# Which instruction carries a wait: the last store's and the kernel's end's waits rearranged on SyncE in a row-sum kernel

## The chip, the cores and the metric

One core of one Trainium2 chip runs the kernel. The metric is device microseconds of a run. A run's span, as the profile shows it, is some 1.8 us shorter (160.8 us of span at 162.61 us in the profiled run before); only differences matter here. The record marks each run as fast or slow by its time and granted clock; all runs quoted are fast, at a granted clock of 1.0.

The engines that matter are VectorE (DVE in the profile), ScalarE (ACT) and SyncE (SP), which issues every DMA. "SPq" in a profile line is SyncE's sequencer. A nop is an instruction that does no work, used here to carry waits; a drain stands at the kernel's end, where it waits too, and the closing barrier is where all engines meet before the kernel ends.

## The reference

```python
batch, seq, dim = 32, 512, 1024        # x: float32, 64 MiB
def reference(x, multiplier):          # multiplier = 0.5
    return (np.sum(x, axis=-1) * multiplier).astype(np.float32)
```

There are 16384 rows of 1024 numbers in, 16384 numbers out.

## The kernel before

Each of 128 partitions owns 128 rows, handled in 8 blocks of 16. Seven blocks are one 8 MB load each into one of three buffers; VectorE sums half the rows, ScalarE the other half. The last block is loaded in five pieces, so that little work is left when the last bytes land. Results of the first 112 rows per partition (this is the 112-row pitch; it is in both kernels) go out in an early store, the last 16 in a last store. The part that matters is the end:

```python
    cut = 640
    ...                                           # pieces of the last block, the final row in two:
    for lo, hi in ((0, cut), (cut, D)):
        loads.append(nc.sync.dma_start(out=t[:, B - 1, lo:hi], in_=x_last[:, B - 1, lo:hi]))
    nc.sync.dma_start(out=out_rows, in_=res[:, 0:own])          # early store, 112 rows
    on_act = {4, 5, 6, 7, 11, 12, 14}
    for r in range(B - 1):
        ...                                       # ScalarE or VectorE, one row each
    dve_span(t, B - 1, 0, cut, part)              # partial sum of the final row
    dve_span(t, B - 1, cut, D, res[:, rows - 1 : rows], start=part)   # the last sum

    seen = nc.sync.nop()                          # waits for the loads and the last ScalarE row
    for i in loads[-8:] + acts[-1:]:
        tc.add_manual_dep(seen.ins, i.ins.name, ...Sync..., reason="ends seen early")
    store = nc.sync.dma_start(out=out_last, in_=res[:, own:])   # last store, 16 rows
    tc.add_manual_dep(store.ins, seen.ins.name, ...NoSync..., reason="in this order")
```

An instruction that depends on several others must wait for several semaphores. In the built program each instruction carries at most one or two waits, and the others stand in separate semaphore instructions ahead of it. The Trainium skill, "Perfetto Trace Analysis", section "Identifying Dependency Chains", says that such instructions may be inserted; this program agrees: six stand between the early store and the last one. It matters which wait stands where, because the program puts them there by its own order, not by which ends last. The end of SyncE's program before, each wait in brackets:

```
semaphore instr.  [load 5]
semaphore instr.  [load 6] [load 4]
semaphore instr.  [load 7] [last load]
semaphore instr.  [ScalarE's last row] [load 2]
semaphore instr.  [VectorE's last sum] [load 1]     <- the wait that ends last
semaphore instr.  [load 5] [load 0]
last store        [ScalarE's last row]
branch
semaphore instr.  [last store landed] [early store landed]
drain             [VectorE's last sum]
drain             enters the closing barrier of all engines
```

(A load is numbered by its semaphore. The pieces of the last block use the first loads' semaphores again, so loads 0, 1 and 2 stand here for pieces of the last block that land before the last load.)

## Time and profile before

| | before |
|---|---|
| median of the first three runs | 162.62 us (162.53 to 162.68) |
| moved by DMA | 67.18 MB, mean 418 GB/s |
| VectorE, ScalarE busy | 42%, 42% |
| chain that ended last | loads of x 86%, VectorE's reductions 11% |

First the table of stretches (core 0; length, busy us of each engine and its number of instructions, clock, DMA share, GB/s):

```profile
40.00:80.00 40.00, 17.75 (x5) 16.85 (x32) 0.00 (x0) 1.00 1.03 446
80.00:120.00 40.00, 18.71 (x5) 17.80 (x33) 0.00 (x0) 1.00 0.97 420
...
157.90:160.80 2.90, 0.50 (x4) 0.00 (x0) 0.00 (x0) 1.00 0.03 3
```

The 16 DMA engines are full, so the loads set the pace up to 157.9 us. The Trainium skill, "Perfetto Trace Analysis", section "Roofline", gives about 435 GB/s as what the 16 DMA engines of a core move together; this trace's mean of 418 GB/s is near it. (The 446 GB/s and the share of 1.03 in one stretch come from the view's counting a packet whole where it starts; with each packet spread over its own time, the trace gives 434 GB/s and a share of 1.00 there.) In the last 2.9 us almost nothing is moved: VectorE is busy for half a microsecond of it, and the DMA share is 0.03.

The timeline of that tail (start us, duration us, engine, line, operation, operands, count):

```profile
157.47 0.49 DVE L65 CUSTOM_DVE_ANT_0 xb<-xb 128x320 f32<-128x320 f32 x1
...
157.89 0.08 DVE L65 DVE_READ_ACCUMULATOR2_ANT part<- 128x1 f32 x1
158.02 0.42 DVE L65 CUSTOM_DVE_ANT_0 xb<-xb,part 128x192 f32<-128x192 f32 x1
158.37 0.08 DVE L65 DVE_READ_ACCUMULATOR2_ANT res<- 128x1 f32 x1
158.60 0.34 SPq L129 DMA_DIRECT2D out_dram<-res  x1
```

VectorE is done at 158.45, the store starts at 158.60. The instructions of the store's own line say what lies between (duration in ns as min/median/max, first and last start):

```profile
L129 SPq EVENT_SEMAPHORE  x2: 28/28/28, 158.5 to 158.5; - x2
L129 SPq DMA_DIRECT2D out_dram<-res x1: 344/344/344, 158.6 to 158.6; - x1
```

Two semaphore instructions stand behind VectorE's end. The view of SyncE's waits shows the wait that ends last at the kernel's end (us, times, longest):

```profile
SPq L194 <- DMA out_dram<-res: 1.1, 1, 1.1
...
SPq L129 <- DVE res L65: 0.5, 1, 0.5
```

The views print hundredths of a microsecond or tenths; the trace's records hold nanoseconds. They are given in tables below, in us from the span's start. A "start" is the record of an instruction's start, an "increment" or "landing" the record of the semaphore event.

### The profile page before, as it was taken

What the parts mean: (1) busy time and instruction counts of PE and PEld (TensorE: products, weight loads), DVE (VectorE), ACT (ScalarE), POOL (GpSimd) and SP (SyncE); (2) the same over time, 40 slices, a digit from 0 to 9 for tenths busy, and PEclk for the clock granted to TensorE, in tenths of its full rate; (3) what the DMA queues carried; (4) which work ended last, traced back from release to release, by engine and by line L of the source; (5) the groups of instructions that cost most, each with busy time, mean ns of one, the idle gap of its engine ahead of it and who ended that gap; (6) DMA issues with size and microseconds to landing.
All of it is one profiled execution on the core that took longest, in us unless ns stands there. A gap on an engine that the chain in (4) does not pass through costs nothing.

```text
span 160.8 us, 236 instructions
## 1 busy us (share of the span) xinstructions
DVE 68.1 (42%) x34; ACT 67.9 (42%) x127; POOL 0.2 (0%) x4
## 2 busy tenths in 40 slices
DVE  0000059600794009920199002990049700597453
ACT  3000059500793009910099002980039700596952
POOL 0000000000000000000000000000000000000000
DMA  7996996996996996996996996996996996998990
GB/s 261 522 522 261 522 522 261 522 522 261 522 522 261 522 522 261 522 522 261 522 524 261 522 505 277 522 505 277 522 505 277 522 489 293 408 489 381 413 390 23
DMA packets 2017, 67.18 MB, mean 418 GB/s; under 512 B 480, under 2 KB 608, under 8 KB 736
## 3 DMA queue, kind: packets, MB, share of 16 engines
q1 hardware_dynamic: 2016, 67.18, 97.3%
q14 instruction: 1, 0.01, 0.0%
HBM read 67.11 MB, written 0.07 MB: 418 GB/s over the span
## 4 chain that ended last, share of the span: by engine, by line
DMA 86%; DVE 11%; SPq 1%; issue 0%; DVEq 0%
DMA xb<-in_x_dram 86%; DVE sums L81 11%; SPq L99 1%; DVE xb L65 1%; SPq L79 0%; DVE part L65 0%; DVEq L194 0%
## 5 line engine op out<-in xcount | busy, mean ns | idle before, releaser
L55 ACT ACTIVATE xb<-xb 128x1024 f32<-128x1024 f32 x63 | 65.6, 1042 | 88.2 <-DMA xb<-in_x_dram 88.2
L81 DVE TENSOR_REDUCE sums<-xb 128x8 f32<-128x8192 f32 x7 | 60.8, 8686 | 85.0 <-DMA xb<-in_x_dram 85.0
L55 ACT ACTIVATION_READ_ACCUMULATOR xb<-xb 128x1 f32 x63 | 11.8, 187 | 0.0
L65 DVE CUSTOM_DVE_ANT_0 xb<-xb 128x512 f32<-128x512 f32 (+1 forms) x9 | 5.6, 667 | 5.1 <-DMA xb<-in_x_dram 4.9
L55 ACT ACT_TABLE_LOAD x1 | 1.3, 1283 | 1.7 <-PEq L180 1.7
L84 DVE TENSOR_SCALAR res<-sums 128x8 f32<-128x8 f32 x7 | 1.2, 171 | 0.2
L65 DVE DVE_READ_ACCUMULATOR2_ANT res<- 128x1 f32 x9 | 0.7, 83 | 0.0
L65 DVE CUSTOM_DVE_ANT_0 xb<-xb,part 128x192 f32<-128x192 f32 x1 | 0.4, 419 | 0.1
L180 POOL MEMSET const-bfloat16-1.0<- 128x1 bf16 x1 | 0.1, 101 | 0.0
L180 POOL MEMSET const-uint8-127<- 128x1 uint8 x1 | 0.1, 101 | 0.0
L180 POOL MEMSET const-float32-0.0<- 128x1 f32 x1 | 0.1, 98 | 0.2 <-issue 0.2
L180 POOL MEMSET const-float32-1.0<- 128x1 f32 x1 | 0.1, 98 | 0.0
L65 DVE DVE_READ_ACCUMULATOR2_ANT part<- 128x1 f32 x1 | 0.1, 83 | 0.0
## 6 DMA issues: line engine op xcount, KB each, us to landing
xb<-in_x_dram SPq DMA_DIRECT2D x1, 4096.0 KB, 39.6
xb<-in_x_dram SPq DMA_DIRECT2D x1, 2560.0 KB, 45.4
xb<-in_x_dram SPq DMA_DIRECT2D x1, 1024.0 KB, 47.4
xb<-in_x_dram SPq DMA_DIRECT2D x1, 320.0 KB, 47.7
xb<-in_x_dram SPq DMA_DIRECT2D x1, 192.0 KB, 47.7
xb<-in_x_dram SPq DMA_DIRECT2D x7, 49.6
out_dram<-res SPq DMA_DIRECT2D x1, 56.0 KB, 10.8
out_dram<-res SPq DMA_DIRECT2D x1, 8.0 KB, 1.4
```

Source lines behind the costliest of these rows:

```text
L55: acts.append(nc.scalar.activation(out=t[:, r, :], in_=t[:, r, :], func=mybir.ActivationFunctionType.Copy, scale=mul, accum_out=res[:, col ...
L65: nc.vector.tensor_tensor_reduce(out=t[:, r, lo:mid], in0=t[:, r, lo:mid], in1=t[:, r, mid:hi], scale=mul, scalar=start, op0=ADD, op1=ADD, ...
L81: nc.vector.reduce_sum(out=sums[:, c0 : c0 + h], in_=t[:, 0:h, :], axis=mybir.AxisListType.X)
L84: nc.vector.tensor_single_scalar(out=res[:, c0 : c0 + h], in_=sums[:, c0 : c0 + h], scalar=mul, op=mybir.AluOpType.mult,)
L99: nc.sync.dma_start(out=t[:, lo:hi, :], in_=x_last[:, lo:hi, :])
L180: nc = _bacc.Bacc("TRN2", target_bir_lowering=False, num_devices=1)
```

## The change

Intent: after the wait that ends last, no other instruction should stand on SyncE before the store, and none before the end's drain. The store is told that it need not wait for ScalarE again (the nop in front has), so that VectorE's wait is the one it carries. A second nop, behind the store, takes the end's other waits while the store is on its way.

```diff
+    def nop_after(engine, waits_for, follows):
+        i = engine.nop()
+        for w in waits_for:
+            tc.add_manual_dep(i.ins, w.ins.name, SYNC, reason="end seen here")
+        for f in follows:
+            tc.add_manual_dep(i.ins, f.ins.name, ORDER, reason="in this order")
+        return i
...
-    nc.sync.dma_start(out=out_rows, in_=res[:, 0:own])
+    early = nc.sync.dma_start(out=out_rows, in_=res[:, 0:own])
...
-    dve_span(t, B - 1, cut, D, res[:, rows - 1 : rows], start=part)
-    seen = nc.sync.nop()
-    for i in loads[-8:] + acts[-1:]:
-        tc.add_manual_dep(seen.ins, i.ins.name, ..., reason="ends seen early")
+    final = dve_span(t, B - 1, cut, D, res[:, rows - 1 : rows], start=part)
+    seen = nop_after(nc.sync, loads[-8:] + acts[-1:], [])
     store = nc.sync.dma_start(out=out_last, in_=res[:, own:])
-    tc.add_manual_dep(store.ins, seen.ins.name, ..., reason="in this order")
+    tc.add_manual_dep(store.ins, seen.ins.name, ORDER, reason="in this order")
+    for a in acts[-len(on_act) :]:
+        tc.declare_no_dep(store.ins, a.ins.name, reason="waited for by the nop in front")
+    nop_after(nc.sync, [early, final], [store])
```

The built program's end on SyncE after it:

```
semaphore instr.  [load 5] [load 4]
semaphore instr.  [load 6] [last load]
semaphore instr.  [load 7] [load 2]
semaphore instr.  [ScalarE's last row] [load 1]
semaphore instr.  [load 5] [load 0]
last store        [VectorE's last sum]              <- the wait that ends last
semaphore instr.  [VectorE's last sum]
branch            [early store landed]
drain             [last store landed]               <- the wait that ends last
drain             enters the closing barrier of all engines
```

Everything ahead of this, on all five engines, is the same in both programs.

More of the change, by code (lines that the diff above doesn't have):

```diff
@@ L49 @@
     part = res_pool.tile([P, 1], fp32, name="part")
+    SYNC = mybir.DependencyInfo(mybir.DependencyClass.Sync, mybir.DependencyReason.DATA)
+    ORDER = mybir.DependencyInfo(
+        mybir.DependencyClass.NoSync, mybir.DependencyReason.SCHED_ONLY
+    )
+    def nop_after(engine, waits_for, follows):
[5 more added lines that the diff above has]
+        return i
     loads = []
@@ L64, in dve_span @@
         mid = (lo + hi) // 2
-        nc.vector.tensor_tensor_reduce(
+        return nc.vector.tensor_tensor_reduce(
             out=t[:, r, lo:mid],
@@ L116 @@
     dve_span(t, B - 1, 0, cut, part)
-    dve_span(t, B - 1, cut, D, res[:, rows - 1 : rows], start=part)
-    seen = nc.sync.nop()
-    for i in loads[-8:] + acts[-1:]:
-        tc.add_manual_dep(
-            seen.ins,
-            i.ins.name,
-            mybir.DependencyInfo(mybir.DependencyClass.Sync, mybir.DependencyReason.DATA),
-            reason="ends seen early",
-        )
-    store = nc.sync.dma_start(out=out_last, in_=res[:, own:])
-    tc.add_manual_dep(
-        store.ins,
-        seen.ins.name,
-        mybir.DependencyInfo(mybir.DependencyClass.NoSync, mybir.DependencyReason.SCHED_ONLY),
-        reason="in this order",
-    )
+    final = dve_span(t, B - 1, cut, D, res[:, rows - 1 : rows], start=part)
+    seen = nop_after(nc.sync, loads[-8:] + acts[-1:], [])
+    store = nc.sync.dma_start(out=out_last, in_=res[:, own:])
+    tc.add_manual_dep(store.ins, seen.ins.name, ORDER, reason="in this order")
+    for a in acts[-len(on_act) :]:
+        tc.declare_no_dep(store.ins, a.ins.name, reason="waited for by the nop in front")
+    nop_after(nc.sync, [early, final], [store])
     def start_loads_at_entry(nc_):
```

## The prediction

> **What bounds the kernel.** The page's chain of work gives 86% to the loads of x, 11% to reductions and 1% to the sync queue. 67.18 MB move at a mean of 418 GB/s, and the table of stretches shows a DMA share of 0.97 to 1.03 from 0 to 150 us. VectorE and ScalarE are busy 42% each. The change touches nothing there: the order of instructions is the same on all engines up to the last store, and the 112-row pitch is already in the kernel before. So about 157.9 of the 160.8 us of span cannot move. Only the tail can.
>
> **The tail before**, from the trace's instruction records (us of the span): the last partial sum (128x192, 419 ns) and its accumulator read (83 ns) raise VectorE's semaphore at 158.461. Then, on SyncE: a semaphore instruction carrying that wait starts at 158.477, a second, whose waits were met long ago, at 158.537, the store at 158.604 (344 ns). Its last piece lands at 160.012. A semaphore instruction for both stores' landings starts at 160.029, a drain (waiting for VectorE, long met) at 160.094, the drain that enters the closing barrier at 160.152. The span ends at 160.826.
>
> **What the change does**, by the built program:
> 1. The store drops its repeated wait for ScalarE and itself carries the wait for VectorE. Of six semaphore instructions ahead of it, five remain, none waiting for VectorE. So after VectorE's last increment two semaphore instructions leave the path.
> 2. After the store stand a nop (VectorE, already met) and a branch (early store, already met). They run while the store flies, 1.4 us from issue to landing: no cost. The end's first drain carries the store's landing wait itself, so one semaphore instruction leaves the end.
>
> The last load lands at 157.888; at about 60 ns each (60 and 67 ns start to start in the tail) the waits ahead of the store are done before 158.25, before VectorE.
>
> **Cost.** Step 1: the store should start 17 to 25 ns after VectorE's increment, as the semaphore instruction did (16 ns), instead of 143 ns after: 118 to 126 ns saved. Step 2: one start-to-start of 65 ns. Sum 0.17 to 0.19 us, all on the critical path: 0.11% of the time. The Trainium skill ("Perfetto Trace Analysis", "DMA Instruction — HWDGE") says that a DMA record starts when its semaphores are satisfied, and that a store to HBM can delay its semaphore surprisingly long; this trace agrees with the second, 1.4 us for 8 KB. That delay stays.
>
> **Predicted time:** 162.62 - 0.17 = 162.45 us, range 162.20 to 162.68. Faster by over 2%: 0.005; within 2%: 0.99; slower by over 2%: 0.005.
>
> **What would show it.** Step 1 right: in the sync queue's records only the store follows VectorE's last increment, by near 20 ns (before: 143). Wrong: 60 ns or more. Step 2 right: from last landing to the barrier's drain some 75 ns (before: 140). Everything up to the last load's landing as before, within scatter; the store still about 1.4 us to landing.
>
> **What would make it wrong.** The three runs before spread over 0.15 us, nearly the whole saving; a shift of the loads' pace by 0.1% hides it. If fetching behind the branch, which now waits too, takes over a microsecond, the end gets later. If the waits moved ahead are not done by 158.46, part of step 1 is lost. If a DMA must be decoded after its wait's release, step 1 saves only about 60 ns.

## The result

| | before | after |
|---|---|---|
| median of 6 runs each | 162.61 us (162.53 to 162.73) | 162.45 us (162.25 to 162.61) |
| ratio, 95% interval | | 0.999, 0.9977 to 1.0003 |

A ratio here and below is the record's, of one kernel's fast runs to those of the kernel before in the same rounds; the ratio of the listed medians or means can differ from it by up to 0.0003. The predicted median was met; the interval of these six runs alone still holds 1, so whether the kernel is faster at all is a question for the trace and for more runs.

The profile after, the lines that answer to those above: first the tail of the timeline, then the store's own line, then SyncE's waits.

```profile
157.46 0.49 DVE L78 CUSTOM_DVE_ANT_0 xb<-xb 128x320 f32<-128x320 f32 x1
...
157.88 0.08 DVE L78 DVE_READ_ACCUMULATOR2_ANT part<- 128x1 f32 x1
158.03 0.42 DVE L78 CUSTOM_DVE_ANT_0 xb<-xb,part 128x192 f32<-128x192 f32 x1
158.38 0.08 DVE L78 DVE_READ_ACCUMULATOR2_ANT res<- 128x1 f32 x1
158.49 0.34 SPq L136 DMA_DIRECT2D out_dram<-res  x1
```

```profile
L136 SPq EVENT_SEMAPHORE  x1: 28/28/28, 158.1 to 158.1; - x1
L136 SPq DMA_DIRECT2D out_dram<-res x1: 344/344/344, 158.5 to 158.5; - x1
```

```profile
SPq L199 <- DMA out_dram<-res: 0.9, 1, 0.9
...
SPq L136 <- DVE res L78: 0.4, 1, 0.4
```

VectorE ends 10 ns later than before, and the store starts 0.12 us earlier. The one semaphore instruction left on the store's line starts at 158.1, long before VectorE's end. The last wait, for the store's landing, is 0.9 us instead of 1.1, because the nop and the branch take a part of the flight that SyncE spent waiting before. In nanoseconds, from the trace's records:

| us of the span | before | after |
|---|---|---|
| last load's last piece lands | 157.888 | 157.898 |
| VectorE's last increment | 158.461 | 158.471 |
| semaphore instructions after it start | 158.477, 158.537 | none |
| last store starts | 158.604 | 158.487 |
| last store's last piece lands | 160.012 | 159.897 |
| end's instructions start | 160.029, 160.094 | 159.914 |
| drain into the barrier starts | 160.152 | 159.976 |
| span ends | 160.826 | 160.650 |

From VectorE's increment to the store it is now 16 ns instead of 143: 127 ns less. From landing to the barrier's drain it is 79 ns instead of 140: 61 ns less. The store takes as long to land as before, 1.410 us against 1.408.

### The profile page after: what moved, and what is told of

Its sections match the earlier page's. It is cut to its first block, busy times and chain, and to the rows that moved or that the text cites. A ratio compares the mean times of both kernels' runs of the same rounds, so it can differ in the third digit from the quotient of the medians.

```text
span 160.7 us, 236 instructions
## 1 busy us (share of the span) xinstructions
DVE 68.1 (42%) x34; ACT 67.9 (42%) x127; POOL 0.2 (0%) x4
## 4 chain that ended last, share of the span: by engine, by line
DMA 86%; DVE 11%; SPq 1%; issue 0%; DVEq 0%
DMA xb<-in_x_dram 86%; DVE sums L94 11%; SPq L112 1%; DVE xb L78 1%; SPq L92 0%; DVE part L78 0%; DVEq L199 0%
```

## The experiments

The last load's landing shifts by 0.1 us and more from one run to the next: it lies between 157.757 and 158.070 us in the nine traces. The loads are issued alike in all of these kernels, so a profiled span, or a time, contains that shift. Three of the four stretches below do not contain it at all, and the fourth starts where it ends. They are the measure for every run (all in ns; the last column is from the last load's landing to the span's end):

| kernel | VectorE's increment to store | store to landing | landing to barrier's drain | whole tail |
|---|---|---|---|---|
| before | 143 | 1408 | 140 | 2938 |
| after | 16 | 1410 | 79 | 2752 |
| after, again | 16 | 1416 | 79 | 2756 |
| store's half only | 16 | 1411 | 140 | 2811 |
| end's half only | 143 | 1409 | 79 | 2876 |
| 20 waits behind the last wait | 1113 | 1415 | 75 | 3847 |
| 4 waits ahead of it | 17 | 1414 | 75 | 2758 |
| 20 waits ahead of it | 659 | 1408 | 75 | 3386 |
| swapped waits on VectorE | 17 | 1408 | 79 | 2807 |

My theory: a semaphore instruction takes SyncE about 50 to 67 ns even if its wait was met long ago, and only those behind the wait that ends last are on the path. Rivals: the difference is scatter of the loads; an earlier store only waits longer to land; the nop and the branch cost what they save; a met wait costs nothing, and the gain lies in which semaphore the store names.

### The changed kernel again, and its two halves

The first run repeats the changed kernel with more rounds. No edit.

> The changed kernel once more, beside its halves. Theory (the gain is semaphore instructions taken off the path behind the last wait, at 60 to 67 ns each): the store starts 16 ns after VectorE's last increment, 79 ns from the last landing to the barrier's drain, time 0.17 to 0.19 us under before (ratio 0.9989). Rival (the difference of the medians is the loads' pace or scatter): the ratio moves to 1.000 with more runs.

The second keeps only the store's half:

```diff
-    nop_after(nc.sync, [early, final], [store])
```

> Only the store's half: the store carries VectorE's wait itself, the end is as before. Theory: store 16 ns after VectorE's last increment (before 143), last landing to the barrier's drain as before, 140 ns; 0.127 us under before, ratio 0.9992. Rival (an earlier store only waits longer for its landing): issue to landing grows from 1.41 to about 1.53 us and the gain is 0.

The third keeps only the end's half:

```diff
-    for a in acts[-len(on_act) :]:
-        tc.declare_no_dep(store.ins, a.ins.name, reason="waited for by the nop in front")
```

> Only the end's half: the store as before, the nop behind it carries the early waits of the end. Theory: store 143 ns after VectorE's last increment, last landing to the barrier's drain 79 ns instead of 140; 0.061 us under before, ratio 0.9996. Rival (the branch with its wait costs what the end saves): 0.

| | median (range), 5 runs | ratio, 95% interval |
|---|---|---|
| before, same rounds, 9 runs | 162.61 us (162.48 to 162.82) | |
| after, again | 162.34 us (162.30 to 162.43) | 0.9983, 0.9970 to 0.9997 |
| store's half | 162.42 us (162.35 to 162.62) | 0.9988, 0.9976 to 1.0001 |
| end's half | 162.51 us (162.42 to 162.87) | 0.9995, 0.9983 to 1.0008 |

With more rounds the interval of the changed kernel no longer holds 1, and all five of its runs (up to 162.43 us) lie below all nine of before (from 162.48 us): the scatter rival falls. The halves cannot be told from before by their times alone, since both intervals hold 1; the trace tells them apart to a few ns. The store's half shortens the tail by 2938 - 2811 = 127 ns, the end's half by 2938 - 2876 = 62 ns, the sum of 189 ns against 186 ns for both together. Each half changes its own stretch and leaves the other as it was, and the flight of the store stays at 1.41 us. So neither part is given back later.

The ratio here, 0.9983, is a gain of 0.27 us, more than the 0.186 us of the tail. In this run's trace the last load landed at 157.802 instead of 157.888, which is of the size of the rest; the programs are the same up to there, so I take this for the loads' scatter. It is not shown beyond the one trace per kernel.

### Twenty waits behind the last wait

```diff
-        i = engine.nop()
+        i = engine.nop(nofuse=True)
...
-    seen = nop_after(nc.sync, loads[-8:] + acts[-1:], [])
+    seen = nop_after(nc.sync, loads[-8:], [])
+    seen = nop_after(nc.sync, [final], [seen])
+    for a in acts[-20:]:
+        seen = nop_after(nc.sync, [a], [seen])
```

Each nop waits for another of ScalarE's last 20 rows, all done by then. (First builds, in which all the nops waited for the same thing, were not run: in the built program the repeated waits were gone. The values have to differ. For the added waits, ScalarE also raises its semaphore after more of its rows, here and in the next two runs.)

> The changed kernel with VectorE's wait put back in front and 20 semaphore instructions, each with one wait met long ago, plus one more, between it and the store. Theory: each takes about 47 to 55 ns start to start, so the store starts 1.05 to 1.2 us after VectorE's last increment; about 163.55 us, ratio to before 1.0055 to 1.0062. Rival (a wait already met costs nothing, the gain came from which semaphore the store itself names): the store starts within 0.2 us, time as before.

Measured: median 163.50 us (163.41 to 163.65, 4 runs), ratio 1.0054, interval 1.0041 to 1.0068. The timeline's last lines and the line of the nops:

```profile
158.49 0.08 DVE L78 DVE_READ_ACCUMULATOR2_ANT res<- 128x1 f32 x1
159.69 0.34 SPq L139 DMA_DIRECT2D out_dram<-res  x1
```

```profile
L57 SPq EVENT_SEMAPHORE  x26: 17/17/10158, 147.8 to 160.1; - x26
```

The store starts 1113 ns after VectorE's increment. The first semaphore instruction starts 16 ns after the increment, and 22 starts follow (20 nops, the store's own semaphore instruction, the store), so (1113 - 16) / 22 = 49.9 ns each on average. The record of a nop is only 17 ns long: two thirds of its cost lie between the records. A met wait is not free, and the rival that holds it so falls.

### Waits ahead of the last wait

The same nops without the one for VectorE ahead of them, once with 4 and once with 20:

```diff
-    seen = nop_after(nc.sync, loads[-8:] + acts[-1:], [])
+    seen = nop_after(nc.sync, loads[-8:], [])
+    for a in acts[-20:]:                       # acts[-4:] in the first of the two
+        seen = nop_after(nc.sync, [a], [seen])
```

> The changed kernel with 3 semaphore instructions more (8 from the last load's landing on to the store, four of them single waits for ScalarE) ahead of the store, none waiting for VectorE. Theory (what stands ahead of the last wait is free while it ends before it): the last of them starts about 0.2 us before VectorE's last increment, the store 16 ns after it, time as the changed kernel, 162.3 to 162.5 us. Rival (every instruction on SyncE lengthens the end, wherever it stands): 4 times 50 ns more, 162.55 to 162.7 us.

> The same with 20 single waits ahead. Theory: 20 times 50 ns, less the slack of some 0.3 to 0.4 us between the end of the waits and VectorE's last increment; the store starts 0.6 to 0.75 us after that increment and the time is 163.0 to 163.15 us. Were all 20 paid, as behind the last wait, it would be 163.4 to 163.5 us; were waits ahead free without limit, 162.4 us.

(The first text says 3 more; by the built program it is 4, nine semaphore instructions ahead of the store instead of five.)

Measured, with before at 162.58 us (162.48 to 162.76, 9 runs) in the same rounds: with 4, median 162.38 us, ratio 0.9990 (0.9978 to 1.0003, 5 runs); with 20, median 163.10 us, ratio 1.0033 (1.0019 to 1.0046, 4 runs). SyncE's waits show the difference. First with 4, then with 20, all that stands in each view from the loads' wait on ("PEq" is the closing barrier's wait for the other engines, and the last line belongs to the kernel's start):

```profile
SPq L57 <- DMA xb<-in_x_dram: 10.2, 1, 10.2
SPq L201 <- DMA out_dram<-res: 1.0, 1, 1.0
SPq L201 <- PEq L201: 0.6, 2, 0.4
SPq L138 <- DVE res L78: 0.2, 1, 0.2
SPq L187 <- PEq L187: 0.2, 1, 0.2
```

```profile
SPq L57 <- DMA xb<-in_x_dram: 10.2, 1, 10.2
SPq L201 <- DMA out_dram<-res: 1.0, 1, 1.0
SPq L201 <- PEq L201: 0.6, 2, 0.4
SPq L187 <- PEq L187: 0.2, 1, 0.2
```

With 4, SyncE still waits 0.2 us for VectorE, where the changed kernel waited 0.4: the added instructions used up slack and nothing else. The store starts 17 ns after the increment and the tail is 2758 ns, as in the changed kernel (2752 and 2756). With 20 the line for VectorE is gone: VectorE was done first, and SyncE, still working through its waits, starts the store 659 ns after the increment. Had all been behind the last wait it would be 1113. So in these two runs a wait ahead was free as long as SyncE reached the store before the last wait ended.

From the landing to the barrier's drain these two runs and the one with 20 behind took 75 ns, not 79. In their traces no branch with a wait stands behind the store. The two drains of the end follow each other by 58 ns in the five traces without a waiting branch and by 62 or 63 ns in the four with one; what causes these 4 ns was not tested.

### The same recipe on VectorE

The last sum of VectorE also has two waits: the last load, in a semaphore instruction ahead, and the partial sum, carried by itself. This run swaps them.

```diff
-    dve_span(t, B - 1, 0, cut, part)
+    first = dve_span(t, B - 1, 0, cut, part)
+    ready = nop_after(nc.vector, [first], [])
     final = dve_span(t, B - 1, cut, D, res[:, rows - 1 : rows], start=part)
+    tc.declare_no_dep(final.ins, first.ins.name, reason="waited for by the nop in front")
+    tc.add_manual_dep(final.ins, ready.ins.name, ORDER, reason="in this order")
```

> The same recipe tried on VectorE: in the changed kernel the last sum has a semaphore instruction for the last load (landing 157.90) ahead of it and itself carries the wait for the partial sum (157.97), and starts 0.106 us after that semaphore instruction. Here they are swapped: a nop on VectorE waits for the partial sum, the last sum carries the load's wait. Theory (the wait that ends last belongs into the instruction itself; the one ahead costs its start to start after it ends): the last sum starts about 0.11 to 0.13 us after the partial sum's increment instead of 0.06, so 0.05 to 0.07 us later, 162.4 to 162.55 us. Rival (the load's semaphore instruction is what holds it up, and carrying it in the instruction frees the path): the start moves up by some 0.04 us.

Measured: median 162.50 us (162.46 to 162.62, 5 runs), ratio 0.9998 (0.9984 to 1.0011). Its chain of work at the end:

```profile
157.93 0.03 issue
157.96 0.02 DVEq L57
157.98 0.09 issue
158.06 0.42 DVE xb L78
```

The semaphore instruction on VectorE ("DVEq L57") starts 27 ns after the partial sum's increment at 157.929, and the last sum 106 ns after that, at 158.062: 133 ns after the increment, a little over what was expected. In the changed kernel it was 61 ns (157.971 to 158.032). The tail is 2807 ns, 55 ns longer than the 2752 of the changed kernel. So the order that the kernel already has is the better one. The runs also show that this order is not free: in the eight other traces the last sum starts 106 to 112 ns after the semaphore instruction for the load, and 23 to 84 ns after the partial sum's increment. All eight fit a start that is the later of two: some 106 ns after the load's semaphore instruction, or some 23 ns after the partial sum. In the repeat of the changed kernel both fall together: 106 ns after the one (157.829 to 157.935) and 23 ns after the other (157.912).

No run pointed to a version faster than the changed kernel. It is the fastest of those tried, together with the one with 4 more waits ahead, which differs from it by at most 6 ns in any of the four stretches.

## Why the prediction was right

1. "Only the tail can" move. Right. Up to the last load's landing the two programs are equal, and the first trace after shows it at 157.898 against 157.888 us.
2. Step 1, "118 to 126 ns saved", the store "17 to 25 ns after VectorE's increment". Measured 16 ns and 127 ns, each 1 ns outside what was stated. The open question in it, whether a DMA must still be decoded after its wait is released, is answered: 16 or 17 ns in all five traces in which the store carries the last wait and SyncE was there before it ended, as short as for a semaphore instruction, and the store's flight is no longer than before. The Trainium skill, "Perfetto Trace Analysis", section "DMA Instruction — HWDGE (DVE, Sync)", lets a DMA's record start when its semaphores are satisfied; the traces agree.
3. Step 2, "one start-to-start of 65 ns". Measured 61 ns in the changed kernel and 61 ns in the end's half alone, because the two drains now follow each other by 62 ns instead of 58.
4. "They run while the store flies ... no cost." Right: in the changed kernel the branch starts at 158.931 and takes 33 ns, and SyncE then waits 0.9 us for the landing. The feared delay behind the branch does not occur.
5. "The waits ahead of the store are done before 158.25." Right: the last of them starts at 158.081. The run with 4 waits ahead shows that more would have fitted, the one with 20 what happens when they don't.
6. "That delay stays." Right: 1.408 to 1.416 us from issue to landing in all nine traces. The Trainium skill, "DMA: Bandwidth & Descriptors", section "Anatomy of one DMA — SWDGE (gpsimd) path", says that on that other path a DMA's fixed cost is mostly completion, not setup. This store goes by the hardware path, and the records of its DMA packets divide it otherwise, alike in all nine traces: the first packet starts 0.84 us after the store's start (0.34 us of it are the issue's record), the last one ends at 1.05 us, and the last increment comes 0.36 to 0.37 us after that. So most of the 1.41 us passes before anything moves, and of the delay behind the write, which the prediction named with the whole 1.4 us, there is at most 0.37 us.
7. The sum: 0.17 to 0.19 us predicted, 0.176 us off the profiled span and 0.186 us off the tail. The time of 162.45 us was met by the first six runs to the last digit; the five later ones, at 162.34 us, show that this exactness is luck within the scatter of 0.1 us. That scatter was named as what could hide the gain, and in the first six runs it nearly did. The stated range, 162.20 to 162.68 us, would have held with no gain at all (162.62 us); what tested the mechanism are the two stretches of steps 1 and 2.

## What to carry to other kernels

Look at the last wait of the chain that ends last and ask what stands between its end and the instruction that it releases. If other waits stand there, move them ahead, and let the instruction carry the wait that ends last: a semaphore instruction on SyncE cost 50 to 67 ns behind it, and nothing ahead of it as long as there was slack. The gain here was 0.19 us, 0.1% of a kernel of 160 us; whether it is the same in kernels of other lengths was not run. Where it is so small, measure it from a fixed event in the trace, not from the time alone.

## What the Trainium skill lacked or had wrong

- No page gives the cost of a semaphore instruction whose wait is already met (the nearest, "Advanced Engine Details and Errata", section "Network/Comms", has a time for reading a semaphore's value from a sequencer, not for this). On SyncE it took 49.9 ns start to start with one wait (mean of 22), 59 to 67 ns with two; on VectorE the last sum started 106 to 112 ns after the one ahead of it. It belongs to "Perfetto Trace Analysis", section "Sequencer-only Instruction (DRAIN, etc)".
- The same section says that a record starts when all semaphores are satisfied. For a semaphore instruction with two waits the traces show otherwise: it starts when the wait that it names first is met and lasts until the second is met too. In the kernel before, one starts at 148.034, 17 ns after load 7 has landed, and is 9877 ns long, to 157.911, 23 ns after the last load has landed; its fellows are 17 to 28 ns. That it is the first named, not the first met, shows in the one for VectorE and load 1: load 1's wait was met at 156.598, and the record starts at 158.477, 16 ns after VectorE's increment. The line of the nop in the profile before:

```profile
L121 SPq EVENT_SEMAPHORE  x4: 17/28/9877, 147.7 to 157.9; - x4
```

- "Identifying Dependency Chains" on that page says that semaphore instructions may be inserted ahead, but not that the wait left in the instruction itself need not be the one that ends last. Here that was worth 127 ns at the store.
- "DMA: Bandwidth & Descriptors", section "Anatomy of one DMA — SWDGE (gpsimd) path", has its fixed cost, about 2 us, for the software path. For the hardware path the page has a time to the first byte, but none from issue to landing. A store of 8 KB by the hardware path took 1.408 to 1.416 us from issue to landing in all nine traces, 0.84 us of it before its first packet.
